# A pair's transposed activations in a bank of the down products' pool, between the two halves of the next rows' transposes

## The chip, the core and the metric

The kernel runs on one core of one Trainium2 chip. The metric is the device time of one execution in microseconds (us); the median of three runs is compared. TensorE is called PE here, VectorE DVE, ScalarE ACT, GpSimd POOL and SyncE SP, as in the profile. PE's weight loads have a row of their own (PEld).

## The reference, cut to what matters

One inference step of two trunk layers over 640 tokens (512 latent tokens, 128 context tokens) of width 1024. Each layer mixes tokens (attention, pooling, convolution) and then runs a layer of 16 experts, which the change is about. Each expert picks the tokens that it scores highest: 64 of the 512 latent tokens and 16 of the 128 context tokens. In fp32:

```
cap = CAPACITY_FACTOR * T // N_EXPERTS
aff = jax.nn.softmax((u @ w_router).astype(jnp.float32), axis=-1)
g, idx = lax.top_k(aff.swapaxes(1, 2), cap)
xs = jax.vmap(lambda ub, ib: ub[ib])(u, idx)
hdn = (jax.nn.silu(jnp.einsum('becd,edf->becf', xs, w_gate))
       * jnp.einsum('becd,edf->becf', xs, w_up))
ye = jnp.einsum('becf,efd->becd', hdn, w_down) * g[..., None].astype(u.dtype)
```

The rows of ye are then added up at their tokens' places. w_gate and w_up of an expert are 1024 x 512, w_down is 512 x 1024; the three are 6 MB an expert, read once for both token sets.

## The kernel before

The experts run in pairs, eight pairs (j = 0 to 7) in each of the two layers. A pair's latent rows fill 128 partitions (64 of each expert). Its weights are twelve loads of 1024 KB (L1077), which SP issues into a ring of 16 buffers: wg and wu in two halves each, then wd. A load waits until the buffer's last products are done.

PE's work of a pair, in the order in which `experts` (L1056) writes it for the middle pairs (1 to 6):

- `lat(0)` (L1141): the gate and up products (ps_g, ps_u) of the latent rows, first half of the 1024 input features;
- `context` (L1148): both products of the context rows (ps_gc);
- `lat(1)`: the second half of the latent products;
- `load_x` (L1099) for the next pair: `gather` (L960) brings its rows by an indirect DMA of POOL's queue into a row buffer (xsl), and `transpose8` (L248) turns them in two halves of four transposes each (tr). Each half has a PSUM bank, and `modulate` (L257) reads it out into xT, two of its blocks on ACT (L261) and two on DVE (L264);
- `ctx_turn` (L1167): four transposes of the context activations hc (ps_hcT), copied to hcT by ACT;
- `lat_transpose` (L1194): four transposes of the latent activations h (ps_hT), copied to hT, one half by ACT (L1199), the other by DVE (L1200). h comes out of `lat_hidden` (L1187): SiLU of ps_g on ACT, times ps_u on DVE (L1191);
- `ctx_rows` (L1175): the context down products (ps_dc), read out by DVE into yc (L1184);
- `lat_down` (L1203): the latent down products in two halves (ps_d), each read out by DVE into ye (L1212).

yc and ye are scattered with addition by indirect DMAs of POOL's queue (L1110). Pair 0 computes its context part before its latent rows are there and has no `ctx_turn` at its end. Pair 7 has no next rows.

The order on PE is written out: `inline` (L236), through which `mm` and `turn1` go, ties each instruction behind the one before. On the other engines a planner puts the instructions in an order when the program is built, by a simulated timeline; each engine then runs its own in that order.

PSUM has eight banks. `ps_t` (L73) has two, which `ptr` (L111) gives in turn, and both halves of the next rows and ps_hT come from it. `Banks` (L95) gives a pool's banks in turn: three for ps_g, ps_u and ps_gc (L1059), and two, `ps_dn` (L777), for the down products ps_dc and ps_d. One more bank, `pmisc`, holds ps_hcT. A bank that is given again is written once the readers of its last contents are done.

Of the kernel before, what the change touches and what calls it, by code (L numbers as in the profile page):

```python
# [10 lines left out]
F32 = mybir.dt.float32  # L11
# [10 lines left out]
P = 128  # L22
# [5 lines left out]
KD = 8  # L28
# [37 lines left out]
def kernel(ctx: ExitStack, tc: tile.TileContext, a: dict):  # L66
    nc = tc.nc
# [13 lines left out]
    def opool(name, side="left", bufs=1, space=None):  # L81
        kw = dict(name=name, bufs=bufs, reuse_waits="tile")
        if space is not None:
            kw["space"] = space
        else:
            kw["side"] = side
        p = tc.alloc_tile_pool(**kw)
        open_pools[name] = p
        return p
# [21 lines left out]
    def ptr(name):  # L111
        return ps_t.tile([P, 512], F32, tag="tr", name=name)

    def pmisc(name):
        return ps_m.tile([P, 512], F32, tag="misc", name=name)
# [6 lines left out]
    ident = const.tile([P, P], F32, name="ident")  # L122
# [113 lines left out]
    def inline(op, *args, **kw):  # L236

        with tc.issue_after(line["pe"].ins) if line else ExitStack():
            line["pe"] = op(*args, **kw)  # L239
        return line["pe"]  # L240

    def mm(*args, **kw):
        return inline(nc.tensor.matmul, *args, **kw)

    def turn1(*args):
        return inline(nc.tensor.transpose, *args)

    def transpose8(src, emit, psum=ptr, turn=nc.tensor.transpose):  # L248

        for g in range(2):  # L250
            ps = psum("tr8").rearrange("p (k n) -> p k n", k=4)
            for kk in range(4):
                ins = turn(ps[:, kk, :], src[:, 512 * g + kk:512 * g + 512:4], ident)
            emit(g, ps)
        return ins

    def modulate(out, ps, A, B, r, g, on_act=(1, 3)):  # L257
        for kk in range(4):
            k = 4 * g + kk
            if kk in on_act:  # L260
                nc.scalar.activation(out=out[:, kk, :], in_=ps[:, kk, :], func=AF.Identity,  # L261
                                     scale=A[:, r, k:k + 1], bias=B[:, r, k:k + 1])
            else:
                nc.vector.tensor_scalar(out=out[:, kk, :], in0=ps[:, kk, :], scalar1=A[:, r, k:k + 1],  # L264
                                        scalar2=B[:, r, k:k + 1], op0=ALU.mult, op1=ALU.add)
# [694 lines left out]
    def gather(x, src, idx):  # L960
        ins = nc.gpsimd.indirect_dma_start(out=x, out_offset=None, in_=src,  # L961
                                           in_offset=bass.IndirectOffsetOnAxis(ap=idx, axis=0))
        order.setdefault("gather", ins)
        order["last"] = ins
        return x
# [90 lines left out]
    def experts(l, A, B, ctxr, ln, gates, newrow, newhalf, residual, xc, route_late, ps_dn, preload, start_next, finish, keep):  # L1056
# [41 lines left out]

        def load_x(j):  # L1099
            x = gather(newrow("xsl"), zrow[:, :], lgi[:, j:j + 1]) if j else x_first  # L1100
            xT = xp.tile([P, KD, P], F32, tag="xT", name="xT", bufs=2)
            transpose8(x, lambda g, ps: modulate(xT[:, 4 * g:4 * g + 4], ps, A, B, 0, g),
                       turn=turn1 if j else nc.tensor.transpose)
            return xT

        def scatter(acc, y, idx, j):

            for h in range(2):
                hs = slice(64 * h, 64 * h + 64)
                nc.gpsimd.indirect_dma_start(out=acc[:, :], out_offset=bass.IndirectOffsetOnAxis(ap=idx[h][0:64, j:j + 1], axis=0),  # L1110
                                             in_=y[hs], in_offset=None, compute_op=ALU.add)
# [10 lines left out]
        for j in range(NPAIR):  # L1122
# [25 lines left out]
            def context(ks):  # L1148

                for k in ks:  # L1150
                    for q in range(4):
                        i, nm = q // 2, "gu"[q % 2]
                        ins = mm(pc[32 * q:32 * q + 32, :], lhsT=xc[:, k, 16 * es[i]:16 * es[i] + 32],
                                 rhs=w[nm, i, k // 4][:, k % 4, :], start=(k == 0), stop=(k == KD - 1))
                return ins

            def ctx_hidden(after=None):
                sc = newhalf("sc")
                hc = newhalf("hc")[0:64]
                for i in range(2):  # L1160
                    nc.scalar.activation(out=sc[64 * i + 32:64 * i + 64], in_=pc[64 * i:64 * i + 32], func=AF.Silu)  # L1161
                    with tc.issue_after(after.ins) if after else ExitStack():
                        nc.vector.tensor_tensor(out=hc[32 * i:32 * i + 32], in0=pc[64 * i + 32:64 * i + 64],  # L1163
                                                in1=sc[64 * i + 32:64 * i + 64], op=ALU.mult)
                return hc

            def ctx_turn(hc):  # L1167
                hcT = wk.tile([P, 4, 64], F32, tag="hcT", name="hcT", bufs=1)
                pt = pmisc("ps_hcT")[:, 0:256].rearrange("p (k n) -> p k n", k=4)
                for k in range(4):  # L1170
                    turn1(pt[:, k, :], hc[:, 256 * (k // 2) + k % 2:256 * (k // 2) + 256:2], ident[0:64, 0:64])
                nc.scalar.copy(out=hcT, in_=pt)  # L1172
                return hcT

            def ctx_rows(hcT, pd=None):  # L1175
                if pd is None:
                    pd = ps_dn.tile("ps_dc")
                for f in range(4):
                    for q in range(4):
                        i, n = q // 2, q % 2  # L1180
                        mm(pd[32 * q:32 * q + 32, :], lhsT=hcT[:, f, 32 * i:32 * i + 32],
                           rhs=w["d", i, f // 2][:, f % 2, n * 512:n * 512 + 512], start=(f == 0), stop=(f == 3))
                yc = newhalf("yc") if j == NPAIR - 1 else wk.tile([P, 512], F32, tag="yc", name="yc", bufs=2)
                nc.vector.scalar_tensor_tensor(out=yc, in0=pd, scalar=cg[:, j:j + 1], in1=gc2, op0=ALU.mult, op1=ALU.mult)  # L1184
                return yc
# [7 lines left out]

            def lat_transpose(h):  # L1194
                hT = wk.tile([P, 4, P], F32, tag="hT", name="hT", bufs=1)
                pt = ptr("ps_hT").rearrange("p (k n) -> p k n", k=4)
                for k in range(4):
                    turn1(pt[:, k, :], h[:, 256 * (k // 2) + k % 2:256 * (k // 2) + 256:2], ident)
                nc.scalar.copy(out=hT[:, 0:2], in_=pt[:, 0:2])  # L1199
                nc.vector.tensor_copy(out=hT[:, 2:4], in_=pt[:, 2:4])  # L1200
                return hT
# [11 lines left out]
                return ye  # L1213

            if j:
                xT = x_next
            if j == 0:
                quads = list(range(KD))

                def fill(n, after=None):  # L1220
                    ks = [quads.pop(0) for _ in range(min(n, len(quads)))]
                    with tc.issue_after(after.ins) if after else ExitStack():
                        return context(ks)

                (lgi, lso, lg, llast), x_first = route_late(fill)
                xp = opool(f"xT{l}", "left")
                scatter(yaccc, ctx_rows(ctx_turn(ctx_hidden(order["lgi"]))), csi, j)
                xT = load_x(0)
                for t in (1, 2, 3):
                    residual(t, order["last"].ins if t == 3 else None)  # L1230
                lat(0)
                lat(1)
                h = lat_hidden()
                x_next = load_x(j + 1)
                hT = lat_transpose(h)
            elif j < NPAIR - 1:
                lat(0)
                context(range(KD))
                hc = ctx_hidden()
                lat(1)  # L1240
                h = lat_hidden()
                x_next = load_x(j + 1)
                hcT = ctx_turn(hc)
                hT = lat_transpose(h)
                scatter(yaccc, ctx_rows(hcT), csi, j)
            else:
                lat(0)
                lat(1)
                h = lat_hidden()
                context(range(4))  # L1250
                hT = lat_transpose(h)
                context(range(4, 5))
# [118 lines left out]
    xp = opool("x0", "left")  # L1371
# [20 lines left out]
    with tc.high_priority():  # L1392
        ps = ptr("ps_ab").rearrange("p (k c) -> p k c", k=4)
# [7 lines left out]
    A, B = AB[:, 1], AB[:, 0]  # L1401
# [17 lines left out]
    for l in range(depth):  # L1419
# [4 lines left out]
        A, B, ctxr, ln, gates, newrow, newhalf, late, xc, route_late, ps_dn = out_proj(l, mixA, mixC, *rest)  # L1424
# [116 lines left out]
```

## Time and profile before

| | |
|---|---|
| median of three runs | 1296.16 us |
| lowest, highest run | 1294.45, 1302.5 us |
| profiled execution | 1294.52 us |
| its span, first to last instruction | 1292.7 us |
| mean granted clock of PE | 0.966 |
| PE busy | 1193.2 us, 92% |
| PEld busy | 710.7 us, 55% |
| DVE busy | 543.7 us, 42% |
| ACT busy | 368.3 us, 28% |
| POOL busy | 252.8 us, 20% |
| moved by DMA | 342.34 MB, mean 265 GB/s |

The profile is of one execution. Its time is the span and 1.8 us around it. The pairs of layer 0 lie at about 370 to 640 us of the span, those of layer 1 at about 980 to 1260 us. An engine's busy time is the time in which one of its instructions runs; matmuls overlap, since they are pipelined. The granted clock is the share of PE's full clock that the chip gave it.

### The profile page before, as it was taken

What the parts mean: (1) busy time and instruction counts of PE and PEld (TensorE: products, weight loads), DVE (VectorE), ACT (ScalarE), POOL (GpSimd) and SP (SyncE); (2) the same over time, 40 slices, a digit from 0 to 9 for tenths busy, and PEclk for the clock granted to TensorE, in tenths of its full rate; (3) what the DMA queues carried; (4) which work ended last, traced back from release to release, by engine and by line L of the source; (5) the groups of instructions that cost most, each with busy time, mean ns of one, the idle gap of its engine ahead of it and who ended that gap; (6) DMA issues with size and microseconds to landing.
All of it is one profiled execution on the core that took longest, in us unless ns stands there. A gap on an engine that the chain in (4) does not pass through costs nothing.

```text
span 1292.7 us, 18180 instructions
## 1 busy us (share of the span) xinstructions
PE 1193.2 (92%) x7244; PEld 710.7 (55%) x7244; DVE 543.7 (42%) x1266; ACT 368.3 (28%) x800; POOL 252.8 (20%) x234
## 2 busy tenths in 40 slices
PE   5999999999879999999969999999987999999994
PEld 1877886987523333333349998798752333333331
DVE  1554464777531121111297756477653111111116
ACT  1532134663411110111145423475341101011111
POOL 0210002004330221121175000200433022012114
PEclk8999999999979999999989999999998999999998
DMA  9868666164869999999543315606487999999932
GB/s 360 310 209 301 226 237 226 69 214 150 339 259 402 397 396 406 410 400 332 193 138 98 86 46 197 242 19 225 157 320 287 406 396 396 410 406 386 357 102 82
DMA packets 85078, 342.34 MB, mean 265 GB/s; under 512 B 18713, under 2 KB 32089, under 8 KB 54401
## 3 DMA queue, kind: packets, MB, share of 16 engines
q1 hardware_dynamic: 73568, 305.96, 61.4%
q0 software_dynamic: 9840, 29.45, 8.4%
q10 hardware_dynamic: 1584, 5.77, 1.1%
q8 instruction: 57, 0.93, 0.3%
q14 instruction: 29, 0.23, 0.1%
HBM read 313.73 MB, written 27.51 MB: 264 GB/s over the span
## 4 chain that ended last, share of the span: by engine, by line
PE 84%; DVE 7%; ACT 4%; DMA 2%; issue 1%; SPq 1%; POOL 0%; POOLq 0%; ACTq 0%; DVEq 0%
PE ps_d L239 9%; PE ps_g L239 9%; PE ps_u L239 9%; PE ps_gc L239 8%; PE ps_dc L239 5%; PE ps_ada L185 4%; PE ps_c L230 3%; PE ps_c L232 3%; PE ps_c L231 3%; PE ps_o L231 3%; PE ps_o L230 3%; PE ps_o L232 3%; PE ps_p L733 1%; PE tr L239 1%; PE ps_b L230 1%
## 5 line engine op out<-in xcount | busy, mean ns | idle before, releaser
L239 PE MATMUL ps_g<-wg,xT 128*64 128x512 f32 x512 | 116.1, 595 | 0.1
L239 PE MATMUL ps_d<-wd,hT 128*64 128x512 f32 x512 | 113.6, 595 | 2.5 <-DVE yc L1184 1.6
L239 PE MATMUL ps_u<-wu,xT 128*64 128x512 f32 x512 | 115.4, 592 | 0.0
L239 PE MATMUL ps_gc<-wu,xc 128*32 128x512 f32 x512 | 115.0, 595 | 0.0
L239 PE MATMUL ps_gc<-wg,xc 128*32 128x512 f32 x512 | 115.0, 594 | 0.0
L1161 ACT ACTIVATE sc<-ps_gc 32x512 f32<-32x512 f32 x32 | 18.8, 587 | 328.8 <-PE ps_gc L239 299.7
L1163 DVE TENSOR_TENSOR hc<-ps_gc,sc 32x512 f32<-32x512 f32 x32 | 22.0, 688 | 174.9 <-ACT sc L1161 174.8
L239 PEld LDWEIGHTS ps_d<-wd,hT 128*64 128x64 f32 x512 | 35.5, 137 | 78.7 <-issue 75.7
L1110 POOL DMA_INDIRECT yaccc<-yc,csi x28 | 39.8, 1421 | 192.5 <-DVE yc L1184 155.0
L239 PEld LDWEIGHTS ps_g<-wg,xT 128*64 128x64 f32 x512 | 36.0, 137 | 75.1 <-issue 72.7
L239 PEld LDWEIGHTS ps_u<-wu,xT 128*64 128x64 f32 x512 | 37.2, 137 | 72.6 <-issue 71.8
L239 PE MATMUL ps_dc<-wd,hcT 128*32 128x512 f32 x512 | 71.1, 705 | 0.9 <-ACT hcT L1172 0.9
L239 PEld LDWEIGHTS ps_gc<-wg,xc 128*32 128x32 f32 x512 | 29.2, 110 | 75.0 <-issue 73.7
L185 PE MATMUL ps_ada<-wada,cs 128*32 128x512 f32 x368 | 60.1, 630 | 4.8 <-DMA wada<-in_w_ada_dram 4.8
L1212 DVE SCALAR_TENSOR_TENSOR ye<-ps_d,lg,gl 128x512 f32<-128x512 f32 x32 | 24.0, 751 | 95.7 <-PE ps_d L239 92.9
L1191 DVE TENSOR_TENSOR h<-ps_u,sg 128x512 f32<-128x512 f32 x16 | 11.1, 692 | 104.1 <-PE ps_u L239 104.1
L261 ACT ACTIVATE xT<-tr,modB,modA 128x128 f32<-128x128 f32 x64 | 28.0, 459 | 60.8 <-DVE xT L264 59.1
L239 PEld LDWEIGHTS ps_dc<-wd,hcT 128*32 128x32 f32 x512 | 17.2, 126 | 43.0 <-issue 39.1
L961 POOL DMA_INDIRECT xsl<-zrow,lgi x16 | 15.9, 991 | 102.3 <-PE tr L239 87.9
L285 POOL TENSOR_TENSOR bsd<-bsd,neg_half 128x1 f32<-128x1 f32 x15 | 9.5, 634 | 128.7 <-DVE bsd L284 128.7
L1184 DVE SCALAR_TENSOR_TENSOR yc<-ps_dc,cg,gc 128x512 f32<-128x512 f32 x16 | 12.0, 749 | 52.9 <-PE ps_dc L239 52.9
L227 POOL TENSOR_TENSOR wo00l<-r_wo,wo00h 128x1024 fp32r<-128x1024 f32 x4 | 10.4, 2610 | 119.4 <-ACT wo00h L226 119.4
(618 smaller groups left out, 2839.0 us busy)
## 6 DMA issues: line engine op xcount, KB each, us to landing
wg<-in_w_gate_dram SPq DMA_DIRECT2D x64, 1024.0 KB, 12.4
wu<-in_w_up_dram SPq DMA_DIRECT2D x64, 1024.0 KB, 14.9
wd<-in_w_down_dram SPq DMA_DIRECT2D x64, 1024.0 KB, 17.8
wada<-in_w_ada_dram SPq DMA_DIRECT2D x46, 1024.0 KB, 7.2
r_wo<-in_w_out_dram SPq DMA_DIRECT2D x8, 1024.0 KB, 8.7
zrow<-xa ACTq DMA_DIRECT2D x8, 512.0 KB, 7.7
yacc<-xa POOLq DMA_DIRECT2D x8, 512.0 KB, 9.9
z<-yacc SPq DMA_DIRECT2D x8, 512.0 KB, 6.2
```

The lines of the kernel that those rows point to most:

```text
L185: nc.tensor.matmul(ps[32 * j:32 * j + 32, :], lhsT=cs[:, k, :], rhs=w[:, j * 512:(j + 1) * 512], start=(k == 0), stop=(k == KD - 1))
L230: nc.tensor.matmul(out, lhsT=lh, rhs=rh, start=first, stop=False)
L231: nc.tensor.matmul(out, lhsT=lh, rhs=rl, start=False, stop=False)
L232: nc.tensor.matmul(out, lhsT=ll, rhs=rh, start=False, stop=last)
L239: line["pe"] = op(*args, **kw)
L261: nc.scalar.activation(out=out[:, kk, :], in_=ps[:, kk, :], func=AF.Identity, scale=A[:, r, k:k + 1], bias=B[:, r, k:k + 1])
L733: nc.tensor.transpose(pt[:, kk, i * P:(i + 1) * P], prs[i][:, (k0 + kk) * P:(k0 + kk + 1) * P], ident)
L961: ins = nc.gpsimd.indirect_dma_start(out=x, out_offset=None, in_=src, in_offset=bass.IndirectOffsetOnAxis(ap=idx, axis=0))
L1110: nc.gpsimd.indirect_dma_start(out=acc[:, :], out_offset=bass.IndirectOffsetOnAxis(ap=idx[h][0:64, j:j + 1], axis=0), in_=y[hs], in_offset ...
L1161: nc.scalar.activation(out=sc[64 * i + 32:64 * i + 64], in_=pc[64 * i:64 * i + 32], func=AF.Silu)
L1163: nc.vector.tensor_tensor(out=hc[32 * i:32 * i + 32], in0=pc[64 * i + 32:64 * i + 64], in1=sc[64 * i + 32:64 * i + 64], op=ALU.mult)
L1212: order["ye"] = nc.vector.scalar_tensor_tensor(out=ye[:, hs], in0=pd, scalar=lg[:, j:j + 1], in1=gl2[:, hs], op0=ALU.mult, op1=ALU.mult)
```

## The change

`transpose8` loses the argument that chose how its transposes are tied. `load_x` only issues the gather and names the tile for xT; the transposes and the modulation of one half are a function of their own, `turn_x`, whose transposes are always tied into PE's written order. In a middle pair the first half comes behind `ctx_turn`, then `lat_transpose`, then the second half. ps_hT takes a bank of `ps_dn` in place of one of `ps_t`. In pair 0 both halves of the next rows stay ahead of `lat_transpose`, and the first rows' transposes are tied into the order too. Nothing is computed differently.

```diff
-    def transpose8(src, emit, psum=ptr, turn=nc.tensor.transpose):
+    def transpose8(src, emit, psum=ptr):
...
-                ins = turn(ps[:, kk, :], src[:, 512 * g + kk:512 * g + 512:4], ident)
+                ins = nc.tensor.transpose(ps[:, kk, :], src[:, 512 * g + kk:512 * g + 512:4], ident)
...
         def load_x(j):
             x = gather(newrow("xsl"), zrow[:, :], lgi[:, j:j + 1]) if j else x_first
-            xT = xp.tile([P, KD, P], F32, tag="xT", name="xT", bufs=2)
-            transpose8(x, lambda g, ps: modulate(xT[:, 4 * g:4 * g + 4], ps, A, B, 0, g),
-                       turn=turn1 if j else nc.tensor.transpose)
-            return xT
+            return x, xp.tile([P, KD, P], F32, tag="xT", name="xT", bufs=2)
+
+        def turn_x(x, xT, g):
+            ps = ptr("tr8").rearrange("p (k n) -> p k n", k=4)
+            for kk in range(4):
+                turn1(ps[:, kk, :], x[:, 512 * g + kk:512 * g + 512:4], ident)
+            modulate(xT[:, 4 * g:4 * g + 4], ps, A, B, 0, g)
...
             def lat_transpose(h):
                 hT = wk.tile([P, 4, P], F32, tag="hT", name="hT", bufs=1)
-                pt = ptr("ps_hT").rearrange("p (k n) -> p k n", k=4)
+                pt = ps_dn.tile("ps_hT").rearrange("p (k n) -> p k n", k=4)
...
             if j:
-                xT = x_next
+                xT = x_next[1]
...
-                xT = load_x(0)
+                xs0 = load_x(0)
+                xT = xs0[1]
+                turn_x(*xs0, 0)
+                turn_x(*xs0, 1)
...
                 x_next = load_x(j + 1)
+                turn_x(*x_next, 0)
+                turn_x(*x_next, 1)
                 hT = lat_transpose(h)
             elif j < NPAIR - 1:
...
                 x_next = load_x(j + 1)
                 hcT = ctx_turn(hc)
+                turn_x(*x_next, 0)
                 hT = lat_transpose(h)
+                turn_x(*x_next, 1)
                 scatter(yaccc, ctx_rows(hcT), csi, j)
```

## Rows read from the trace of the kernel before

**Rows 1.** The page: busy us of an engine, share of the span, instructions.

```profile
PE 1193.2 (92%) x7244; PEld 710.7 (55%) x7244; DVE 543.7 (42%) x1266; ACT 368.3 (28%) x800; POOL 252.8 (20%) x234
```

**Rows 2.** Waits, whole span: engine, line, waited for: total us, times, longest us.

```profile
PE ps_hT L239 <- ACT xT L261: 17.6, 14, 1.5
...
PE ps_d L239 <- DVE yc L1184: 1.6, 1, 1.6
...
PEld ps_hT L239 <- ACT xT L261: 19.6, 14, 1.7
```

**Rows 3.** Timeline, end of pair 0, layer 0: start, us, instructions [idle before <-releaser].

```profile
387.37 1.86 ACT L261 ACTIVATE xT<-tr,modB,modA 128x128 f32<-128x128 f32 x4 [1.40 <-DVE xT L264]
388.81 0.55 PEld L239 LDWEIGHTS ps_hT<-ident,h 128*128 128x128 f32 x4 [1.66 <-ACT xT L261]
...
389.59 0.37 ACT L1199 COPY hT<-ps_hT 128x256 f32<-128x256 f32 x1 [0.37 <-PE ps_hT L239]
```

**Rows 4.** Timeline, end of pair 2, layer 0.

```profile
453.10 1.05 PEld L239 LDWEIGHTS tr<-ident,xsl 128*128 128x128 f32 x8 [0.81 <-issue]
...
453.32 0.69 DVE L1191 TENSOR_TENSOR h<-ps_u,sg 128x512 f32<-128x512 f32 x1 [4.38 <-PE ps_u L239]
453.93 1.34 DVE L264 TENSOR_SCALAR xT<-tr,modA,modB 128x128 f32<-128x128 f32 x3
454.27 0.55 PEld L239 LDWEIGHTS ps_hcT<-ident,hc 64*128 64x128 f32 x4
...
454.36 0.46 ACT L261 ACTIVATE xT<-tr,modB,modA 128x128 f32<-128x128 f32 x1 [3.95 <-DVE xT L264]
455.05 0.37 ACT L1172 COPY hcT<-ps_hcT 128x256 f32<-128x256 f32 x1 [0.23 <-PE ps_hcT L239]
455.32 1.40 ACT L261 ACTIVATE xT<-tr,modB,modA 128x128 f32<-128x128 f32 x3
...
456.18 0.55 PEld L239 LDWEIGHTS ps_hT<-ident,h 128*128 128x128 f32 x4 [1.36 <-ACT xT L261]
...
456.86 0.16 PEld L239 LDWEIGHTS ps_dc<-wd,hcT 128*32 128x32 f32 x8
```

**Rows 5.** Chain that ended last, middle pairs: start us, us, work.

```profile
421.70 3.57 PE ps_dc L239 x32
...
456.93 3.57 PE ps_dc L239 x32
...
492.25 5.13 PE ps_dc L239 x32
...
1177.40 5.27 PE ps_dc L239 x32
```

**Rows 6.** Stretches: us; busy PE, PEld, DVE, ACT, POOL; granted clock, DMA share, GB/s.

```profile
386.20:390.00 3.80, 1.89 (x12) 1.50 (x12) 2.24 (x6) 2.20 (x5) 0.36 (x1) 1.00 1.02 388
390.00:393.40 3.40, 3.38 (x16) 1.20 (x18) 0.42 (x1) 0.00 (x0) 0.00 (x0) 1.00 1.02 419
...
456.90:460.40 3.50, 3.50 (x33) 0.90 (x32) 0.42 (x1) 0.37 (x1) 0.00 (x0) 1.00 1.00 414
...
492.20:495.60 3.40, 3.40 (x21) 0.88 (x24) 0.42 (x1) 0.37 (x1) 0.00 (x0) 0.53 1.01 426
```

**Rows 7.** Timeline, DVE, start of pair 2, layer 0.

```profile
432.36 0.75 DVE L1212 SCALAR_TENSOR_TENSOR ye<-ps_d,lg,gl 128x512 f32<-128x512 f32 x1 [2.65 <-PE ps_d L239]
```

**Rows 8.** DMA: SP's issues; wd's us to landing; loads' queue 417:600 (packets, MB, share).

```profile
414.58 5.06 SPq L1077 DMA_DIRECT2D wd<-in_w_down_dram  x4
...
wd<-in_w_down_dram SPq DMA_DIRECT2D x4, 1024.0 KB, 20.8
...
558.80 4.24 SPq L1077 DMA_DIRECT2D wd<-in_w_down_dram  x4
...
wd<-in_w_down_dram SPq DMA_DIRECT2D x4, 1024.0 KB, 13.9
...
q1 hardware_dynamic: 9068, 66.03, 87.1%
```

## The prediction

> **What bounds the kernel now.** I read the page's busy shares first: TensorE (PE) is busy for 92% of the span [rows 1], so what can be won is its idle time and what a lower clock costs it. Next I read the waits by their sums. In the expert stages one stands out: the transposes of a pair's activations (ps_hT) wait for ScalarE's modulation of the next rows (xT). It comes 14 times, which is pairs 0 to 6 in two layers: 17.6 us by the matmul row, 19.6 us by the row of the weight loads, which start a matmul [rows 2]. With 1.66 us for each pair 0 [rows 3] the twelve middle pairs have (19.6 - 3.3) / 12 = 1.36 us each.
>
> The timeline of one pair's end shows why. The eight transposes of the next rows (tr) start at 453.10, the four of the context activations (ps_hcT) at 454.27, and the last of these weight loads ends at 454.82. The activations h were ready at 454.01 (453.32 + 0.69). Yet ps_hT starts at 456.18, after 1.36 us, because its bank is one of the two that hold the halves of the next rows, and ScalarE still reads that one [rows 4]. The wait is for a bank, not for data.
>
> The chain of waits shows a second cost. The 32 context down products (ps_dc) behind this wait take 3.57 us in six of the twelve middle pairs and 5.13 to 5.27 us in the other six [rows 5]. The granted clock tells why: 1.00 throughout behind one wait, 0.53 over 3.4 us behind another, mostly the 1.2 GHz level instead of 2.4 [rows 6]. PE did the same ahead of both: transposes, 1.4 us of nothing, transposes.
>
> **The change part by part.**
>
> *ps_hT moves to the down products' pool.* The last reader of its bank is then the product of the pair before, at 432.36 + 0.75 for the pair shown [rows 7], over 20 us earlier. So that wait goes. This pool now gives four tiles a pair instead of three: ps_hT shares a bank with the first ps_d, ps_dc with the second. The first ps_d now needs both copies of hT finished, which it reads anyway; the second needs yc read out, as before. ScalarE's copy of its half of hT takes 0.37 us [rows 3], VectorE's comes behind it, and the 3.57 us of ps_dc lie between. Nothing new is on the path.
>
> *The two halves are moved.* New order on PE: ps_hcT, first half, ps_hT, second half, ps_dc. By the starts of the weight loads the eight take 1.17 us, ps_hcT half of that, 0.59, and ps_hT 0.68 (456.18 to 456.86): 2.44 us in place of 3.76 (453.10 to 456.86) [rows 4]. h must be there when ps_hT starts, at 453.10 + 0.59 + 0.59 = 454.28; it is, at 454.01. What is late next: ps_dc, at about 455.5, needs hcT, whose source is done about 453.9 and whose copy takes 0.37. It fits. A middle pair gains between 1.32 (3.76 - 2.44) and 1.36; I take 1.35. Twelve of them: **16.2 us**.
>
> *The modulations of the second half* (two on VectorE at 0.45, two on ScalarE at 0.47 [rows 4]) end around 456.9. The next pair's first products read them, 10.6 us after ps_dc began (421.70 to 432.3 [rows 5, 7]), so about 466: 9 us of cover. The gather stays at its place in the program, and the moved step issues no DMA. But a row buffer is released by the last transpose, 1.2 us later relative to the first one; a gather on POOL's queue that waits for this buffer, and the scatters queued behind the gather, move by as much. They have most of a pair to land, so zero; without that cover, 1.2 us a pair.
>
> *Pair 0.* Here hT's copy stands behind four ScalarE modulations, which end at 389.23, and starts at 389.59 [rows 3]. If it keeps its place in ScalarE's queue the gain is 0.36 us; if it is put first, up to the whole wait of 1.66. The program's order speaks for the first: 2 x 0.36 = **0.7 us**, at most 3.3. The eight transposes of the first rows join PE's written order behind ps_dc, where they also stand now: zero.
>
> *Pair 7* has no next rows. Its ps_hT changes the bank alone, and the joins after it find the same two banks in turn (28 tiles before them, 36 now): zero.
>
> *The clock.* Without the stop, the stretch without a product is 2.4 us of transposes back to back. Nothing in the trace shows exactly that. Bounds: all six slow stretches stay (0), or all go: 1.56 + 5 x 1.70 = **10.0 us** (5.13 and 5.27 against 3.57) [rows 5]. The nearest row is the end of pair 0: from 386.20 to 390.00 PE ran twelve transposes with two stops and no product, and the granted clock was 1.00 there and in the 3.4 us that follow [rows 6]. The new stretch is shorter and fuller than that one, so I take 10.0.
>
> *Transfers.* This is the resource that a faster PE runs into. Their share in the four stretches of [rows 6] is 1.00 to 1.02: they are full. The four wd loads issued from 414.58 landed 20.8 us later (median), those issued from 558.80 only 13.9: four pairs in 137.3 us, 34.3 us each [rows 8]. A pair on PE without a slow stretch took 35.23 (421.70 to 456.93) [rows 5], so it will take 33.9, a little under the transfers' 34.3. The loads would fall behind by 0.4 us a pair, 2.6 in a layer. The first wd loads land at 435.4 and the last, issued by 419.64, at 440.4; both are needed from 456.93 on, 16 us later. So this costs nothing, but the slack is gone.
>
> **Sum.** 16.2 + 0.7 + 10.0 = 26.9. The profiled execution took 1294.52 us (span 1292.7), 1.64 under the median of the three runs. 1294.5 - 26.9 = 1267.6; I say **1268** for the new median, 2.2% under the old one. I don't add the 1.64: the runs scatter upwards, which one or a few more slow stretches in a run would do, and those go.
>
> **Rivals.**
>
> 1. *The stop goes, the slow stretches stay.* Only 16.9 is won: 1277.6. For it: PE still runs no product for 2.4 us at each pair. Against it: the end of pair 0 [rows 6]. The Trainium skill (TensorE: Matmul & The Clock Gate, Part 4: PE-mode transpose) states that transposes don't count as PE-busy; by that rule the stretch would still look idle, though a third shorter, and some drops would stay. This trace, with 1.00 behind 3.8 us of transposes and stops, does not bear the rule out. Chance 0.13.
>
> 2. *Transfers become the bound.* By the bytes between 417 and 600 us (66.03 MB on the loads' queue [rows 8]) a pair's twelve loads of 1024 KB take 34.9 us, 1.0 over PE's 33.9. It decides once 16 us of lead are used up, by slower scatters or loads. At full price, 12 x 1.0: 1279.6. Chance 0.08.
>
> 3. *yc is read late.* Once, the second ps_d waits 1.6 us for yc [rows 2], which VectorE reads out after ps_dc. The planner sets VectorE's order anew. If all eleven other middle pairs came to this, 11 x 1.6 = 17.6: 1285. It is one pair in twelve now. Chance 0.05.
>
> 4. *Slower.* If ScalarE's queue has hcT's copy behind the modulations of the second half, ps_dc waits for all of it. That half is transposed at about 455.6, and ScalarE's first modulation starts behind VectorE's first, as now (454.36) [rows 4]: 0.45, two of 0.47, the copy of 0.37, so ps_dc starts at 457.36 instead of 456.86. That is 0.50 x 12 = 6.0 more; the stop ahead of ps_dc stays as long as it was, and all twelve pairs may drop instead of six, 10.0 more. 1294.5 + 6.0 + 10.0 - 0.7 = 1309.8; with the six drops of now, 1299.8. It decides from the order alone. Against it: now the copy (455.05) runs ahead of three modulations (455.32) that the program issues before it [rows 4]. Chance 0.05.
>
> 5. *No effect*, because ps_hT finds something else to wait for just as long: about 1294. h is ready and the bank free, so 0.03.
>
> **Chances and range.** The forecast holds 0.66. About 1% (13 us) is what a measurement of this kernel can tell from no change. Faster by over 1% (below 1283.2): the forecast and rivals 1 and 2, 0.87, less a little for slower ends of the last two: 0.86. Within 1%: rivals 3 and 5, the lower part of 4: 0.11. Slower by over 1%: the upper end of rival 4, 0.03. The range reaches down to 1263 (all 3.3 of pair 0, and the 1.6 of rival 3 gone as well) and up to 1281, over rivals 1 and 2.
>
> **What would show it.** Right: no wait of ps_hT on xT in the middle pairs; ps_dc 2.4 us after the first transpose; all twelve ps_dc near 3.6 us at granted clock 1.00; a period of 33.9 us; in pair 0, ps_d 0.4 us or more sooner. Wrong: a new wait of ps_dc on hcT, or of ps_d on hT or yc; a granted clock near 0.5 behind the transposes; PE waiting for wg, wu or wd.

## The result and the profile after

The changed kernel's median is 1267.62 us (1264.65 to 1269.12, four runs), against 1295.9 us for the kernel before, run on the same chip (1294.45 to 1302.5, four runs): a ratio of 0.9772 with a 95% interval of 0.9747 to 0.9797. The forecast was 1268. The profiled execution after took 1264.65 us (span 1262.9), the one before 1294.52 (span 1292.7); the mean granted clock rose from 0.966 to 0.978.

The page's first part after, as in [rows 1]. PE lost 13 us of busy time for the same 7244 instructions; the other engines hardly changed:

```profile
PE 1180.2 (93%) x7244; PEld 707.2 (56%) x7244; DVE 542.2 (43%) x1266; ACT 367.9 (29%) x800; POOL 252.6 (20%) x234
```

The waits of PE after, in the columns of [rows 2]. No row of ps_hT is left. The wait for yc came once before and comes twice now; that for hT is at the end of pair 0, in both layers:

```profile
PE ps_d L239 <- DVE yc L1187: 3.2, 2, 1.6
...
PE ps_d L239 <- ACT hT L1202: 1.6, 2, 0.8
```

The timeline of the changed kernel at the end of pair 2 in layer 0, the place of [rows 4]:

```profile
449.54 0.55 PEld L239 LDWEIGHTS ps_hcT<-ident,hc 64*128 64x128 f32 x4 [0.81 <-issue]
...
449.74 0.69 DVE L1194 TENSOR_TENSOR h<-ps_u,sg 128x512 f32<-128x512 f32 x1 [4.37 <-PE ps_u L239]
...
450.15 0.56 PEld L239 LDWEIGHTS tr<-ident,xsl 128*128 128x128 f32 x4
...
450.32 0.37 ACT L1175 COPY hcT<-ps_hcT 128x256 f32<-128x256 f32 x1 [3.41 <-PE ps_hcT L239]
450.62 0.57 PEld L239 LDWEIGHTS ps_hT<-ident,h 128*128 128x128 f32 x4
...
451.11 0.58 PEld L239 LDWEIGHTS tr<-ident,xsl 128*128 128x128 f32 x4
...
451.39 0.46 ACT L261 ACTIVATE xT<-tr,modB,modA 128x128 f32<-128x128 f32 x1 [0.70 <-DVE xT L264]
451.75 0.36 ACT L1202 COPY hT<-ps_hT 128x256 f32<-128x256 f32 x1
451.81 0.16 PEld L239 LDWEIGHTS ps_dc<-wd,hcT 128*32 128x32 f32 x8
```

The four groups of transposes follow one another without an idle entry. From the first to ps_dc it is 451.81 - 449.54 = 2.27 us, where it was 3.76. Read what was feared too: h is done at 450.43, 0.19 us ahead of ps_hT, and hcT's copy runs as soon as its source is there, ahead of every modulation.

The granted clock in that stretch and in the 3.6 us behind it, in the columns of [rows 6], is 1.00:

```profile
449.50:451.80 2.30, 2.30 (x18) 2.08 (x16) 1.10 (x2) 0.78 (x3) 0.00 (x0) 1.00 1.01 427
451.80:455.40 3.60, 3.60 (x35) 0.96 (x34) 1.47 (x4) 1.58 (x5) 0.00 (x0) 1.00 1.01 419
```

The chain that ended last, after (start, us, work), as in [rows 5]:

```profile
370.30 1.17 PE tr L239 x8
...
387.89 7.09 PE ps_d L239 x32
...
418.13 3.57 PE ps_dc L239 x32
...
451.88 3.57 PE ps_dc L239 x32
...
553.12 3.57 PE ps_dc L239 x32
...
588.69 3.57 PE ps_dc L239 x32
592.26 7.05 PE ps_d L239 x32
599.31 7.70 DMA wu<-in_w_up_dram
607.06 7.29 DMA wd<-in_w_down_dram
614.40 6.79 DMA wd<-in_w_down_dram
621.24 5.36 PE ps_d L239 x22
...
629.31 2.85 PE ps_z L239 x8
...
967.89 1.17 PE tr L239 x8
...
985.47 7.09 PE ps_d L239 x32
...
1225.57 1.06 PE ps_z L239 x2
```

All twelve ps_dc of the middle pairs take 3.57 us; no slow one is left. A pair takes 33.75 us (418.13 to 451.88). From 553.12 to 588.69 it is 35.57: there the second half of ps_d waits for yc, at 1.82 us in the period. And for 22 us at the end of layer 0 the chain runs through transfers, which it did not before.

The marks of the kernel before, from its chain:

```profile
371.02 1.17 PE tr L253 x8
...
390.02 7.09 PE ps_d L239 x32
...
642.21 1.54 PE ps_z L239 x4
...
982.38 1.17 PE tr L253 x8
...
1001.38 7.09 PE ps_d L239 x32
...
1255.45 1.06 PE ps_z L239 x2
```

Differences of these marks say where the 29.8 us between the two spans came from:

| stretch | before | after | gained |
|---|---|---|---|
| start to pair 0's first rows, layer 0 | 371.02 | 370.30 | 0.72 |
| those rows to pair 0's ps_d | 19.00 | 17.59 | 1.41 |
| ps_d of pair 0 to the joins (ps_z), layer 0 | 252.19 | 241.42 | 10.77 |
| joins to pair 0's first rows, layer 1 | 340.17 | 338.58 | 1.59 |
| those rows to pair 0's ps_d | 19.00 | 17.58 | 1.42 |
| ps_d of pair 0 to the joins, layer 1 | 254.07 | 240.10 | 13.97 |
| joins to the end | 37.25 | 37.33 | -0.08 |

### The profile page after: what moved, and what is told of

Its sections match the earlier page's. It is cut to its first block, busy times and chain, and to the rows that moved or that the text cites. A ratio compares the mean times of both kernels' runs of the same rounds, so it can differ in the third digit from the quotient of the medians.

```text
span 1262.9 us, 18196 instructions
## 1 busy us (share of the span) xinstructions
PE 1180.2 (93%) x7244; PEld 707.2 (56%) x7244; DVE 542.2 (43%) x1266; ACT 367.9 (29%) x800; POOL 252.6 (20%) x234
## 4 chain that ended last, share of the span: by engine, by line
PE 83%; DVE 7%; DMA 4%; ACT 3%; issue 1%; SPq 0%; POOL 0%; POOLq 0%; ACTq 0%; DVEq 0%
PE ps_d L239 9%; PE ps_g L239 8%; PE ps_u L239 8%; PE ps_gc L239 8%; PE ps_dc L239 4%; PE ps_ada L185 4%; PE ps_c L230 3%; PE ps_c L232 3%; PE ps_c L231 3%; PE ps_o L231 3%; PE ps_o L230 3%; PE ps_o L232 3%; DMA r_wA<-in_w_in_dram 1%; PE tr L239 1%; PE ps_p L733 1%
## 5 line engine op out<-in xcount | busy, mean ns | idle before, releaser
L239 PE MATMUL ps_dc<-wd,hcT 128*32 128x512 f32 x512 | 61.0, 618 | 0.9 <-ACT hcT L1175 0.9
L1113 POOL DMA_INDIRECT yacc<-ye,lgi x14 | 19.9, 1418 | 76.9 <-DVE ye L1215 44.4
```

## The experiments

The theory after the result: the stop for the bank is worth 1.48 us in each of the twelve middle pairs (35.23 less 33.75), and with it go the six slow stretches, 10.0 us. The rivals: the new place between the two halves does it, or a part of it; the clock holds for another reason than the missing stop; and transfers, not PE, set the new time.

**The bank alone.** Both halves stand ahead again, as before:

```
-                hcT = ctx_turn(hc)
                 turn_x(*x_next, 0)
-                hT = lat_transpose(h)
                 turn_x(*x_next, 1)
+                hcT = ctx_turn(hc)
+                hT = lat_transpose(h)
```

> The bank alone: ps_hT comes from the down products' pool, but in the middle pairs both halves of the next rows are transposed ahead of ps_hcT and ps_hT, as before the change. Theory (ps_hT waited for a bank, and nothing else): no wait of ps_hT is left, ps_dc starts 2.3 to 2.4 us after the first transpose, hcT's copy is done just in time, and all twelve ps_dc take about 3.6 us; 1266 to 1270 us, the same as the changed kernel. Rival (the place between the two halves is needed too, because hcT's copy then stands behind modulations on ScalarE): ps_dc waits 0.5 to 1.4 us for hcT, 6 to 16 us slower than the changed kernel, 1274 to 1284, and more if the slow stretches come back.

Measured: 1267.66 us (1266.47 to 1269.38), ratio 0.9755 (0.9733 to 0.9778) against a before of 1299.2 on its chip. The same stretch in its timeline:

```profile
453.14 1.05 PEld L239 LDWEIGHTS tr<-ident,xsl 128*128 128x128 f32 x8 [0.81 <-issue]
...
455.60 0.16 PEld L239 LDWEIGHTS ps_dc<-wd,hcT 128*32 128x32 f32 x8
```

It takes 2.46 us, a pair 33.94, and all twelve ps_dc are at 3.57. The rival's wait of ps_dc for hcT came in no middle pair. So the bank carries the change; the place between the halves is worth 0.19 us a pair by the rows, 2.3 us in all, which the medians do not tell apart.

**The order alone.** ps_hT comes from the transposes' pool again:

```
-                pt = ps_dn.tile("ps_hT").rearrange("p (k n) -> p k n", k=4)
+                pt = ptr("ps_hT").rearrange("p (k n) -> p k n", k=4)
```

> The order alone: ps_hcT, first half, ps_hT, second half, but ps_hT's bank comes from the two of the transposes' pool as before. Theory: the bank is the cause, so the wait only moves: the second half now finds its bank still read by the modulations of the first half and waits 0.6 to 1.6 us a middle pair; 1283 to 1298 us by how many slow stretches stay. Rival (the order alone puts enough work between): no wait of PE over 0.2 us at the end of a pair, about 1268 us.

Measured: 1289.78 us (1287.47 to 1290.23), ratio 0.9923 (0.9899 to 0.9948). The row of its waits in which the stop is found again, and from its chain the one slow ps_dc:

```profile
PE tr L239 <- DVE hT L1203: 15.5, 12, 1.3
```

```profile
1102.71 4.71 PE ps_dc L239 x32
```

The stop moves to the second half's transposes and keeps its length (15.5 / 12 = 1.3 us); by this row it is a reader of ps_hT that is waited for, not those of the first half, which the expectation had named. A pair takes 35.30 us, as before. What the run gained is the clock: one slow ps_dc of twelve instead of six. PE does nearly the same as before (twelve transposes, a stop, four transposes), so a stop of this length leads to a drop of the granted clock only at times. What decides it, no run here shows.

**The stop filled.** The kernel before, with nine more transposes of the identity in each middle pair, into a bank that no one reads, where PE stood still:

```
                 hcT = ctx_turn(hc)
+                spare = ps_dn.tile("ps_fill").rearrange("p (k n) -> p k n", k=4)
+                for k in range(9):
+                    turn1(spare[:, k % 4, :], ident, ident)
                 hT = lat_transpose(h)
```

> The kernel before, with nine more transposes (of the identity, into a bank of the down products' pool, read by nobody) between ps_hcT and ps_hT in each middle pair: 9 x 0.146 = 1.31 us of transposes where PE stopped for 1.36 us. ps_hT starts when it did. Theory (the slow stretches come from PE's standing still, and transposes keep the clock up): all twelve ps_dc take about 3.6 us at granted clock 1.00, nothing else moves, 10 us won: 1284 to 1288 us. Rival (transposes count for nothing, as the Trainium skill has it in TensorE: Matmul & The Clock Gate, Part 4: PE-mode transpose): as many slow ps_dc as before, five to eight of twelve at 5.1 to 5.3 us, 1293 to 1299 us.

Measured: 1283.64 us (1281.55 to 1288.28), ratio 0.9876 (0.9853 to 0.99). Its chain, and its granted clock in the stretch and behind it:

```profile
460.66 3.57 PE ps_dc L239 x32
...
495.89 3.57 PE ps_dc L239 x32
```

```profile
456.90:460.60 3.70, 3.61 (x28) 3.06 (x27) 2.24 (x5) 2.00 (x5) 0.00 (x0) 1.00 1.02 430
460.60:464.20 3.60, 3.60 (x35) 0.97 (x34) 0.42 (x1) 0.37 (x1) 0.00 (x0) 1.00 1.02 423
```

The period is 35.23 us as before and the stretch without a product as long, 3.7 us, but PE is busy in 3.61 of it (0.33 us of the stop were left), and all twelve ps_dc take 3.57. One profile alone could be luck, since the order alone had only one slow ps_dc with its stop in place. But the eight profiles here without a stop of over 1 us ahead of a middle pair's ps_dc (the changed kernel twice, and the other six versions) have no slow ps_dc in 96; the three of the kernel before have 18 in 36, and the order alone 1 in 12. So it was PE's standing still that cost the clock, not the time without a product: the two terms of the forecast come apart, and each is there by itself. By the rows of the twelve ps_dc the clock is worth 10.0 us. In this execution the two expert stages (pair 0's ps_d to the joins) got only 7.25 us shorter, because the products behind pair 0's stop, which was not filled, were slow in both layers; it was the slowest of the four runs (1288.28). The medians differ by 15.6 (1299.2 less 1283.64), and where the rest comes from is open. The weight loads of the nine transposes took 0.96 us.

**No pacing of a layer's last loads.** In both kernels the last six loads of a layer (from number 90 of 96) are tied to the landing of the load two before:

```
-PACED = 90
+PACED = 200
```

> The changed kernel without the pace that lets each of the last six weight loads of a layer wait for the landing of the load two before it. Theory (the transfers have no slack left at the end of layer 0, where the second part of pair 7's wd came 1.1 us late): this wait goes and the loads land some us sooner, 0 to 1.5 us won: 1265.5 to 1268 us. Rival (transfers are the bound of the whole stage by now, and the pace only shapes their queue): the wait stays or moves to the rows that are read back at the end of the layer (z), 1268 to 1275 us.

Measured: 1265.61 us (1265.17 to 1266.5), ratio 0.9742 (0.972 to 0.9764). The chain has no transfer at layer 0's end any more, and PE waits for wd nowhere: the wd loads go out from 585.61 on instead of 602.50, and from 600 to 610 us the core's DMA moves 375 GB/s instead of 291. So it was the pace that made them late. The gain, some 2 us, lies inside the intervals.

**yc read out first.** The changed kernel, with VectorE's readout of the first ps_d put behind that of ps_dc in its queue (pairs 1 to 6):

```
-                nc.vector.scalar_tensor_tensor(out=yc, ...
+                order["yc"] = nc.vector.scalar_tensor_tensor(out=yc, ...
...
-                order["ye"] = nc.vector.scalar_tensor_tensor(out=ye[:, hs], ...
+                with tc.issue_after(order["yc"].ins) if j in range(1, NPAIR - 1) else ExitStack():
+                    order["ye"] = nc.vector.scalar_tensor_tensor(out=ye[:, hs], ...
```

> The changed kernel with one order more written out: in the middle pairs VectorE reads yc out before the first ye. In the changed kernel two pairs (one in each layer) have it the other way round, and PE's second ps_d waits 1.6 us there. Theory (VectorE's order alone makes this wait): it goes in both, 3.2 us won at most, of which layer 0's half can be taken back by the late wd of pair 7: 1264.4 to 1266 us, no wait of ps_d on yc. Rival (yc's buffer is still being scattered, so VectorE would stand and ye come late): a wait of ps_d or of the next pair in its place, 1267 to 1272 us.

Measured: 1265.18 us (1263.01 to 1268.75), ratio 0.9755 (0.9733 to 0.9777). The waits for yc are gone, and another has grown:

```profile
PEld ps_d L239 <- DMA wd<-in_w_down_dram: 4.0, 2, 2.9
```

Two pairs at 1.82 would be 3.6 us. In pair 7 of both layers PE then comes too early for wd and gives part of it back. Beside the changed kernel on that chip (1267.7, below) it is 2.5 us lower, with runs that overlap.

**Both.** The changed kernel with the edits of the last two versions.

> The changed kernel with yc read out first and without the pace of the last six loads. If both add up: 2.0 us of the pace (measured 1265.6 against 1267.6) and up to 3.2 of yc, 1262.4 to 1264.5 us. Rival (transfers end layer 0, so whatever PE gains there it waits for at pair 7): 1264.5 to 1266 us, and a wait of ps_d on wd at the end of layer 0.

Measured: 1262.43 us (1259.1 to 1263.14), ratio 0.9735 (0.9714 to 0.9757). Neither wait is left. The changed kernel itself, timed beside it on that chip (below), took 1267.7: this version is 5.3 us faster, and the two sets of runs do not overlap. It is the fastest version here. By the marks of the chains its two expert stages take 238.27 us each, where the changed kernel's profile beside it has 240.64 and 241.68: 5.8 us less, 3.6 of yc and 2.1 of wd, which was late at the end of both layers in that execution (in the first profile after, at the end of layer 0 alone).

**PE made longer again.** The changed kernel, with nine transposes of the identity ahead of ps_hT's in each middle pair, in its own bank:

```
+                for k in range(9 if 0 < j < NPAIR - 1 else 0):
+                    turn1(pt[:, k % 4, :], ident, ident)
```

> The changed kernel with nine more transposes of the identity ahead of ps_hT in each middle pair (into its own bank, overwritten by the real ones): 1.31 us more work of PE a pair, with no stop. It asks what bounds the changed kernel's expert stages. If PE does: 12 x 1.31 = 15.7 us more, less the 1.1 us of pair 7's wait for wd: 1281 to 1284 us; the twelve ps_dc stay at 3.6 us, so this is also the kernel before without its slow stretches. If the transfers do: they go on at their own rate and PE's new work is hidden in part, 1270 to 1278 us.

Measured: 1278.54 us (1277.92 to 1279.26), ratio 0.9861 (0.9832 to 0.9889), 10.8 over the changed kernel on the same chip. From its chain:

```profile
456.47 3.57 PE ps_dc L239 x32
...
491.20 3.57 PE ps_dc L239 x32
```

A pair takes 34.73 us, 0.98 more, and 12 x 0.98 = 11.8. The 2.1 of the changed kernel's late wd come back, because pair 7 no longer waits for it, and a third pair's wait for yc adds 1.8: 11.5, which is also what the two stages got longer. So all that PE is given to do shows in the time: PE still bounds the stages, and the late loads only their ends. The expectation was too high because it took 0.146 us for a transpose, from the rows' transposes; these took 0.109.

**The changed kernel once more**, beside the last three.

> The changed kernel itself once more, on the same chip as the others of this call, for their comparison: 1266 to 1269 us.

Measured: 1267.7 us (1266.62 to 1270.9), ratio 0.978 (0.9757 to 0.9802), as at first.

**The kernel before, twice more**, for the count of its slow stretches.

> The kernel before, unchanged, profiled once more: how many of the twelve ps_dc of the middle pairs are slow in another execution? In the profiled execution of before it was six at 1294.5 us. Theory (the slow stretches are what makes its runs scatter, 1.67 us each): time = 1284.5 + 1.67 x count, give or take 2 us, with a count that differs from run to run. Rival (the count is fixed at six, and the scatter comes from elsewhere): six again, at whatever time.

> The same once more: 1284.5 + 1.67 x count against six at whatever time.

Measured: 1295.44 and 1296.67 us, each with six slow ps_dc of twelve, as in the first profile and as the rival had it. In these two they are the same six (pairs 2, 4 and 5 of layer 0, 2, 4 and 6 of layer 1), in the first profile others (3, 4 and 6, then 2, 4 and 5). From the chain of the first of the two:

```profile
458.55 5.27 PE ps_dc L239 x32
...
495.48 3.57 PE ps_dc L239 x32
```

In [rows 5] the ps_dc at 456.93 is fast and that at 492.25 slow; here it is the other way round. So six was no accident of one execution, and the 10.0 us were a sound term. The forecast supposed that a few more of them make the slower runs. The three profiles, all with six, lie at 1294.5 to 1296.7 us and don't show it; the runs up to 1302.5 us were not profiled. The changed kernel's runs, with none in either profile, scatter too (1264.65 to 1270.9). What does it stays open.

## Why the prediction was right, point by point

The terms against what the profiled executions show:

| term | forecast | measured |
|---|---|---|
| twelve middle pairs, the stop | 16.2 | 17.8 (12 x 1.48) |
| pair 0, twice | 0.7 | 2.8 (1.41 + 1.42) |
| clock behind the stop | 10.0 | 10.0 (4.93 in layer 0, 5.10 in layer 1) |
| yc late a second time | 0 | -1.8 |
| transfers at layer 0's end | 0 | -1.2 |
| stages that the change doesn't touch | 0 | 2.2 (0.72 + 1.59 - 0.08) |
| sum | 26.9 | 29.8 |

*The wait was for a bank.* This held as argued: with another pool's bank it is gone, in whatever order, and with the old bank it only moves.

*A middle pair* was worth 1.48 us instead of 1.35. The forecast's 2.44 us from the first transpose to ps_dc is what the bank alone gave (2.46); the new order is a little shorter (2.27). By the weight loads each group there takes 0.47 to 0.70 us, and why the sum differs by 0.19 is not shown.

*Pair 0* is the term that was mis-sized: 0.36 us forecast, 1.41 measured. The forecast let hT's copy keep its place behind the four ScalarE modulations. The timeline of the changed kernel at that place shows otherwise:

```profile
385.39 1.05 PEld L239 LDWEIGHTS tr<-ident,xsl 128*128 128x128 f32 x8 [0.81 <-issue]
...
386.65 0.93 ACT L261 ACTIVATE xT<-tr,modB,modA 128x128 f32<-128x128 f32 x2 [1.47 <-DVE xT L264]
387.47 0.36 ACT L1202 COPY hT<-ps_hT 128x256 f32<-128x256 f32 x1
387.73 0.82 ACT L261 ACTIVATE xT<-tr,modB,modA 128x128 f32<-128x128 f32 x2
387.89 0.20 PEld L239 LDWEIGHTS ps_d<-wd,hT 128*64 128x64 f32 x4 [0.97 <-ACT hT L1202]
```

The copy stands between two modulations and two more, so ps_d starts 2.50 us behind the first transpose. In the kernel before it was 3.91:

```profile
386.11 1.05 PEld L239 LDWEIGHTS tr<-ident,xsl 128*128 128x128 f32 x8 [0.81 <-issue]
...
390.02 0.20 PEld L239 LDWEIGHTS ps_d<-wd,hT 128*64 128x64 f32 x4 [0.65 <-ACT hT L1199]
```

So the planner did not keep the program's order on ScalarE here. The forecast had seen the same with hcT's copy [rows 4], used it against rival 4, and did not use it here. The bound of 3.3 for both held the 2.8.

*The clock* came out to the tenth, but the row it leaned on was thin. Pair 0's end, with two stops, had kept 1.00 in [rows 6]; in the profiled run with the filled stop the same place stood still for 1.68 us, and the 3.4 us behind it had 0.65 (0.58 in layer 1; in the run of the order alone, 0.65 in layer 0):

```profile
392.60:396.00 3.40, 3.40 (x12) 1.09 (x14) 0.39 (x1) 0.00 (x0) 0.00 (x0) 0.65 1.01 414
```

That row could have been read the other way. The test that was missing is the filled stop, with the count of slow ps_dc over all profiles. Rival 1 falls with it: the Trainium skill (TensorE: Matmul & The Clock Gate, Part 4: PE-mode transpose) says that transposes don't count as PE-busy in the same way; here 3.7 us with 25 transposes and no long stop kept 1.00, and the same length with 16 and a stop did not in six pairs of twelve. For this kernel the measurement decides. It shows that transposes hold the level; whether they alone would raise it from 1.2 GHz, no run here shows.

*Transfers* were put at zero for the 16 us of lead at a pair in mid-layer. Rival 2 in full did not come: a pair takes 33.75 us, and the longer PE showed that PE sets this. But the lead was looked for in the wrong place, and the pace of a layer's last loads was not looked at. PE ends pair 6 of layer 0 14.2 us sooner (599.31 instead of 613.51), while SP's issues of its last loads, first before and then after, go out when they did:

```profile
595.89 3.13 SPq L1077 DMA_DIRECT2D wu<-in_w_up_dram  x2
603.49 9.21 SPq L1077 DMA_DIRECT2D wd<-in_w_down_dram  x4
```

```profile
595.39 4.25 SPq L1077 DMA_DIRECT2D wu<-in_w_up_dram  x2
602.50 12.22 SPq L1077 DMA_DIRECT2D wd<-in_w_down_dram  x4
```

Pair 7's second half waits for the last wd until 621.24, and the stretch from pair 6's last product to ps_z is 30.0 us instead of 28.7 (to 629.31, and to 642.21 before). Without the pace this wait is gone, so the 1.2 us are the price of the pace, not of transfers that could do no more.

*yc late* (rival 3) came in one more pair, not in eleven: 1.8 of its 17.6 us. *Rival 4* did not come: hcT's copy goes first.

*The number.* The forecast of 1268 agrees with the median to 0.4 us, and the profiled gain is 2.9 over the sum. Two undersized gains (3.7 together) stood against two costs put at zero (3.0), and 2.2 us came from stages that the change doesn't touch. Those 2.2 look like scatter: the profiled execution after is the fastest of the changed kernel's ten runs, and in the second profiles of the two kernels the start and the stretch between the layers differ by 0.0 and 0.5 us. So the terms are known to some 2 us each, and the closeness of the sum is partly luck.

## What to carry to other kernels

When an engine waits and its data are long there, ask whose buffer it wants: a tile that shares a rotating pair of banks with tiles that are read out slowly waits for those readers, and a bank from a pool that is free at that time takes the wait away. Here one more late readout of yc (1.8 us) came with the new plan, and one order written out took it back. A stop on TensorE can cost twice, once for itself and once, as behind half of the stops in the kernel before, for the products behind it: look at their granted clock before costing a change that only shortens or fills the stop. When the bound engine gets faster, check the lead of the loads at the end of each stage, where they are issued last, and what in the program ties them, and not the lead in its middle alone.

## What the runs showed of the hardware

- TensorE's level of 2.4 GHz survives a stretch of nothing but transposes (1.00 through 2.3, 2.5 and 3.7 us of them). A stop of 1.36 us among them led to a granted clock of 0.51 to 0.63 over the 3.4 us behind it, mostly the 1.2 GHz level, in six pairs of twelve in each of three executions, not always the same pairs; a stop of 1.3 us in the other order did so (0.65) in one pair of twelve.
- Nine fp32 transposes of the identity, with the identity as the other operand too, made a pair 0.98 us longer, 0.109 each, where the eight of the rows take 1.17, 0.146 each.
- Loads that went out sooner did not land sooner while the transfers were full (share 1.01 to 1.03 from 560 to 600 us): the changed kernel issued pair 7's last wg loads of layer 0 at 575.98 instead of 587.04 us, and the wu loads that are tied to their landing went out at 595.39 instead of 595.89.
